# A gated linear unit over 32 tiles: the first tile's load split into four strided strips

## The chip, the core and the metric

The kernel runs on one core of a Trainium2 chip. Its time is the device time of one execution in microseconds (us). The median of three runs counts. Loads are issued by SyncE (SP), stores by ScalarE (ACT), and both kinds run on the core's 16 DMA engines.

## What is computed

`x` has 8192 rows of 8192 float32 numbers. Each row is cut in two halves, `a` and `b`, and the output has 8192 rows of 4096 numbers:

```python
def reference(x):
    a, b = np.split(x, 2, axis=-1)
    return a * (1 / (1 + np.exp(-b)))
```

That is a sigmoid and a product for each output number. 268.4 MB are read and 134.2 MB are written.

## The kernel before

A tile is 256 rows of `x`. Each of the 128 partitions takes two neighbouring rows (`R = 2`), which lie side by side in memory, so a tile is 128 runs of 64 KB, 8.39 MB in all. There are 32 tiles (`n_tiles`), and the loop of line 51 goes over them once. Two input buffers `x_sb` and two output buffers `o_sb` (`SLOTS = 2`) are used in turn, so even tiles share one pair and odd tiles the other.

For each tile, line 58 issues one load for all 128 partitions on SP's queue. Line 76 takes the sigmoid of the `b` halves in place on ScalarE, line 77 multiplies on VectorE into `o_sb`, and line 70 stores 4.19 MB on ACT's queue. For tiles 1 to 30 there is one sigmoid and one product for the whole tile; tile 0 and tile 31 are worked in four parts, and tile 31 is also stored in four parts of 1 MB. The load of tile i + 2 waits for the product of tile i, which has read the last of that buffer.

Two things stand outside of this order:

- Line 43 issues a small transfer, named `held`, as the first thing on ACT's queue. It reads 16 times 15 pieces of 64 bytes into a buffer `idle` that nothing uses. The stores go into the same queue behind it.
- `_launch_early` (line 99) works on the finished program: it takes the first load that stands on SP's queue and puts it ahead of the barrier with which all engines start.

`_close_on_sync` (line 112) rearranges the closing barrier so that the kernel ends on the completion of the last store. The calls of `implied` take out waits that follow from others.

Of the kernel before, what the change touches and what calls it, by code (L numbers as in the profile page):

```python
# [8 lines left out]
def _tiles(ctx, tc, x, out):  # L9

    nc = tc.nc
    P = nc.NUM_PARTITIONS  # L20
    DEP = mybir.DependencyInfo(mybir.DependencyClass.Sync, mybir.DependencyReason.DATA)
    fp32 = mybir.dt.float32
    SIG = mybir.ActivationFunctionType.Sigmoid

    n_rows, n_cols = x.shape
    half = n_cols // 2
    R = 2
    SLOTS = 2
    n_tiles = n_rows // (P * R)
    x_t = x.rearrange("(n p r) m -> n p (r m)", p=P, r=R)  # L30
    out_t = out.rearrange("(n p r) m -> n p (r m)", p=P, r=R)

    pool = ctx.enter_context(tc.tile_pool(name="io", bufs=1))
    xs = [pool.tile([P, R * n_cols], fp32, name=f"x_sb{k}") for k in range(SLOTS)]
    os = [pool.tile([P, R * half], fp32, name=f"o_sb{k}") for k in range(SLOTS)]

    def implied(later, *earlier):
        for e in earlier:
            tc.declare_no_dep(later.ins, e.ins, reason="follows from the waits that are kept")

    KEEP = 15
    idle = pool.tile([16, KEEP * 32], fp32, name="idle")
    held = nc.scalar.dma_start(
        out=idle.rearrange("p (k m) -> p k m", m=32)[:, :, 0:16],
        in_=x[0:16, 0 : KEEP * P].rearrange("p (k m) -> p k m", m=P)[:, :, 0:16],
    )
    tc.keep_in_program_order(held)

    gone = [{k: [] for k in ("loads", "sigs", "muls", "stores")} for _ in range(SLOTS)]
    last_stores = [[] for _ in range(SLOTS)]  # L50
    for i in range(n_tiles):
        old = gone[i % SLOTS]
        freed = last_stores[i % SLOTS]
        now = {k: [] for k in old}
        rows = xs[i % SLOTS].rearrange("p (r h m) -> p r h m", r=R, h=2)
        packed = os[i % SLOTS].rearrange("p (r m) -> p r m", r=R)

        load = nc.sync.dma_start(out=xs[i % SLOTS], in_=x_t[i])
        implied(load, *old["loads"], *old["sigs"])
        now["loads"].append(load)  # L60

        if 0 < i < n_tiles - 1:
            parts = [(slice(0, R), slice(0, half))]
        else:
            w = half // 2
            parts = [
                (slice(r, r + 1), slice(c * w, (c + 1) * w)) for r in range(R) for c in range(2)
            ]
        def store(cols):
            ins = nc.scalar.dma_start(out=out_t[i, :, cols], in_=os[i % SLOTS][:, cols])  # L70
            now["stores"].append(ins)

        chunks = []
        for k, (r, c) in enumerate(parts):
            b = rows[:, r, 1, c]
            sig = nc.scalar.activation(out=b, in_=b, func=SIG)  # L76
            mul = nc.vector.tensor_mul(out=packed[:, r, c], in0=rows[:, r, 0, c], in1=b)  # L77
            implied(sig, *old["sigs"], *old["muls"], *old["loads"])
            implied(mul, *old["muls"], *old["loads"], *now["loads"])
            by_sigmoid = i % 2 == 1 and len(parts) == 1  # L80
            implied(mul, *(s for s in old["stores"] if by_sigmoid or s not in freed))
            if by_sigmoid:
                for s in freed:
                    tc.add_manual_dep(sig.ins, s.ins.name, DEP, reason="frees the output slot")
            tc.keep_in_program_order(sig)
            now["sigs"].append(sig)
            now["muls"].append(mul)
            chunks.append(slice(r.start * half + c.start, r.start * half + c.stop))
            if i == n_tiles - 1 and k > 0:
                store(chunks[k - 1])  # L90
        store(chunks[-1] if i == n_tiles - 1 else slice(0, R * half))
        for s in now["stores"]:
            implied(s, *old["loads"], *old["sigs"], *old["muls"], *now["loads"], *now["sigs"])
        for k in old:
            old[k] += now[k]
        last_stores[i % SLOTS] = now["stores"]
# [71 lines left out]
@with_exitstack  # L168
def kernel(
    ctx: ExitStack,  # L170
    tc: tile.TileContext,
    x: bass.AP,
    out: bass.AP,
):
    nc = tc.nc
    with ExitStack() as pools:
        _tiles(pools, tc, x, out)
    tc.close()
    tc.compile()
    _launch_early(nc)  # L180
    _close_on_sync(nc)
# [30 lines left out]
```

## Time and profile before

| what | value |
|---|---|
| time, median of 3 runs | 933.45 us (933.36 to 933.45) |
| span of the profiled execution, first to last instruction | 931.9 us |
| what lies around the span (933.45 less 931.9) | 1.55 us |
| bytes moved by DMA, mean rate over the span | 402.68 MB, 432 GB/s |
| VectorE busy | 278.6 us, 30% of the span |
| ScalarE busy | 227.0 us, 24% of the span |
| loads: issue to landing, shortest, median, longest | 22.0, 42.2, 42.5 us |
| stores of 4 MB: issue to landing, median | 42.0 us |

The time of the profiled execution itself is not recorded beside the three runs; it is taken as its span and the 1.55 us around it, that is as the median. An engine's busy time is what it worked, not what it waited. The two compute engines are idle for two thirds of the span or more, and the DMA engines are busy throughout; a load's time from issue to landing holds the time that it stood in line behind another load.

### The profile page before, as it was taken

The numbers are of one execution on the slowest core, as the hardware profiler recorded it, in microseconds if no ns is written. First come the engines' busy times: TensorE is split into PE (matmuls) and PEld (weight loads), VectorE is DVE, ScalarE is ACT, GpSimd is POOL, SyncE is SP. The second block draws the span as 40 slices with busy tenths as digits, with TensorE's granted clock in tenths as the row PEclk, the third lists the DMA queues.
The fourth block names the chain that finished last, engine by engine and source line by source line (L and its number), as shares of the span: only waits on it lengthen the run. The fifth ranks groups of instructions, "written<-read, shape, count | busy, mean of one in ns | idle before, by whom it ended". The sixth has DMA issues, their size and how long they took to land.

```text
span 931.9 us, 249 instructions
## 1 busy us (share of the span) xinstructions
DVE 278.6 (30%) x38; ACT 227.0 (24%) x39; POOL 0.2 (0%) x4
## 2 busy tenths in 40 slices
DVE  0333312333123331133321333213332133321333
ACT  1413332133320333202332023320233202333023
POOL 0000000000000000000000000000000000000000
DMA  9999999999999999999999999999999999999999
GB/s 405 448 408 430 447 428 450 411 464 408 428 450 428 450 409 466 408 428 450 428 450 408 464 411 428 450 425 453 405 459 419 428 450 425 453 405 453 425 428 405
DMA packets 9905, 402.68 MB, mean 432 GB/s; under 512 B 1328, under 2 KB 1328, under 8 KB 1328
## 3 DMA queue, kind: packets, MB, share of 16 engines
q1 hardware_dynamic: 4608, 268.44, 66.6%
q10 hardware_dynamic: 5296, 134.24, 33.4%
q14 instruction: 1, 0.01, 0.0%
HBM read 268.45 MB, written 134.22 MB: 432 GB/s over the span
## 4 chain that ended last, share of the span: by engine, by line
DMA 72%; DVE 15%; ACT 12%; issue 0%; ACTq 0%
DMA x_sb<-in_x_dram 72%; DVE o_sb L77 15%; ACT x_sb L76 12%; ACTq L70 0%; ACTq L76 0%
## 5 line engine op out<-in xcount | busy, mean ns | idle before, releaser
L77 DVE TENSOR_TENSOR o_sb<-x_sb 128x8192 f32<-128x8192 f32 (+1 forms) x38 | 278.6, 7344 | 645.0 <-ACT x_sb L76 645.0
L76 ACT ACTIVATE x_sb<-x_sb 128x8192 f32<-128x8192 f32 (+1 forms) x38 | 225.7, 5950 | 693.2 <-DMA x_sb<-in_x_dram 691.9
L76 ACT ACT_TABLE_LOAD x1 | 1.3, 1283 | 1.2 <-PEq L196 1.2
L196 POOL MEMSET const-bfloat16-1.0<- 128x1 bf16 x1 | 0.1, 102 | 0.0
L196 POOL MEMSET const-uint8-127<- 128x1 uint8 x1 | 0.1, 101 | 0.0
L196 POOL MEMSET const-float32-0.0<- 128x1 f32 x1 | 0.1, 100 | 0.2 <-issue 0.2
L196 POOL MEMSET const-float32-1.0<- 128x1 f32 x1 | 0.1, 98 | 0.0
## 6 DMA issues: line engine op xcount, KB each, us to landing
out_dram<-o_sb ACTq DMA_DIRECT2D x31, 4096.0 KB, 42.0
out_dram<-o_sb ACTq DMA_DIRECT2D x4, 1024.0 KB, 7.9
x_sb<-in_x_dram SPq DMA_DIRECT2D x32, 42.2
idle<-in_x_dram ACTq DMA_DIRECT2D x1, 15.0 KB, 41.4
```

Source lines behind the costliest of these rows:

```text
L76: sig = nc.scalar.activation(out=b, in_=b, func=SIG)
L77: mul = nc.vector.tensor_mul(out=packed[:, r, c], in0=rows[:, r, 0, c], in1=b)
L196: nc = _bacc.Bacc("TRN2", target_bir_lowering=False, num_devices=1)
```

## The change

Tile 0 is loaded by four transfers where there was one. The first takes partitions 0, 8, 16, and so on to 120 (16 of them), the second partitions 4, 12, 20 and so on (16), the third partitions 2, 6, 10 and so on (32), and the fourth all odd partitions (64). Together they cover each partition once. `_launch_early` is unchanged, so it now moves the first of the four ahead of the barrier; the other three are issued behind the barrier, ahead of the load of tile 1. All other tiles are loaded as before.

```diff
-        load = nc.sync.dma_start(out=xs[i % SLOTS], in_=x_t[i])
-        implied(load, *old["loads"], *old["sigs"])
-        now["loads"].append(load)
+        steps = [(0, 1)] if i else [(0, 8), (4, 8), (2, 4), (1, 2)]
+        for at, step in steps:
+            p = slice(at, P, step)
+            load = nc.sync.dma_start(out=xs[i % SLOTS][p], in_=x_t[i, p])
+            implied(load, *old["loads"], *old["sigs"], *now["loads"])
+            now["loads"].append(load)
```

In the compiled program SP's queue gets three more issues, all of them ahead of the load of tile 1. On ScalarE, the first sigmoid of tile 0 waits for one of the four transfers and the loading of the sigmoid's table, which stands just ahead of it, now waits for the other three; before, it waited for none. The order on every other engine is the same, and lines behind the edit move down by three.

## The prediction

> **What bounds the kernel now.** I read the page first, then stretches of the run as a table, then the chain of waits and the timeline at both ends. From the page: the slices of DMA busy time, the queues, and the issues with their time from issue to landing.
>
> ```profile
> DMA  9999999999999999999999999999999999999999
> ...
> DMA packets 9905, 402.68 MB, mean 432 GB/s; under 512 B 1328, under 2 KB 1328, under 8 KB 1328
> ...
> q1 hardware_dynamic: 4608, 268.44, 66.6%
> q10 hardware_dynamic: 5296, 134.24, 33.4%
> ...
> out_dram<-o_sb ACTq DMA_DIRECT2D x31, 4096.0 KB, 42.0
> ...
> idle<-in_x_dram ACTq DMA_DIRECT2D x1, 15.0 KB, 41.4
> ```
>
> The DMA engines are never below nine tenths. q1 carries the loads: 4608 packets are 32 times 144, that is 128 rows of 64 KB and 16 completions for each load, so each of the 16 engines gets eight rows and one completion. q10 carries the stores and the small transfer. The 1328 packets under 512 B are its 240 pieces and 68 issues times 16 completions: a completion is a packet of its own.
>
> The next table is of stretches of the run: length, busy time of the engines, TensorE clock, DMA share, GB/s.
>
> ```profile
> 0.00:1.00 1.00, 0.00 (x0) 0.00 (x0) 0.20 (x4) 1.00 0.19 66
> 1.00:4.00 3.00, 0.00 (x0) 1.28 (x1) 0.00 (x0) 1.00 0.94 328
> ...
> 42.00:71.00 29.00, 8.69 (x1) 7.03 (x1) 0.00 (x0) 1.00 1.00 434
> 71.00:100.00 29.00, 8.69 (x1) 7.03 (x1) 0.00 (x0) 1.00 1.00 434
> 883.00:912.00 29.00, 8.69 (x1) 7.03 (x1) 0.00 (x0) 1.00 1.00 434
> ```
>
> One load and one store together take 29.0 us at a DMA share of 1.00, from the third tile to the last. The only loss that I see is at the start: 66 of 434 GB/s for 1 us and 328 for 3 us, worth 0.85 + 0.73 = 1.6 us. The end of the chain and the timeline's last store:
>
> ```profile
> 870.43 42.14 DMA x_sb<-in_x_dram
> 912.57 0.02 issue
> 912.59 1.92 ACT x_sb L76
> 914.51 0.02 issue
> 914.53 2.31 DVE o_sb L77
> ...
> 916.86 0.34 ACTq L70
> ```
>
> The last load lands at 912.57. What is left to store then is all of tile 30 (issued at 899.38, one product behind the landing of tile 30) and all of tile 31, 8.39 MB, and it takes 931.9 - 912.57 = 19.3 us: 434 GB/s again. So the tail is covered too. The chain names loads, sigmoids and products, but these are only the round trip of one buffer; the sum is made of DMA time. Whatever time the DMA engines lose at the start is added at the end, one for one, and nothing later gives it back.
>
> **The change, part by part.** *The bytes and rows* of tile 0 stay: 128 rows, eight to an engine if each strip is dealt evenly (1, 1, 2 and 4). *Three more issues* take SP 0.33 to 0.37 us each (the range of SP's 32 issues), 1.1 us in all. They stand ahead of the load of tile 1, which is not needed until tile 0 is through at 22 us, and of the load of tile 2, which waits until 32.89. One row is 64 KB on an engine, 2.42 us at 434 GB/s over 16, so the first strip covers the barrier and the second strip's issue. Price 0; without that cover 0.4 us for each issue.
>
> *A shorter first issue* is the gain. The whole tile's issue takes 0.37 us before the DMA can have all its rows; I take 0.3 us of that as won. The bounds are 0 and the whole starting loss of 1.6 us, which is below 0.2% of 933.45 (1.87 us), about what a measurement of this kernel can tell from no change.
>
> *The table load and its new waits.*
>
> ```profile
> 0.78 0.40 ACTq L43 DMA_DIRECT2D idle<-in_x_dram  x1
> 1.20 1.28 ACT L76 ACT_TABLE_LOAD   x1 [1.20 <-PEq L196]
> 22.03 7.31 ACT L76 ACTIVATE x_sb<-x_sb 128x2048 f32<-128x2048 f32 x4 [19.54 <-DMA x_sb<-in_x_dram]
> ```
>
> Now it follows the landing of tile 0, so tile 0's sigmoids, products, its store and the load of tile 2 (now at 32.9) come 1.3 us later. Queued behind the waiting instruction are only those and the later stores. The load of tile 2 is needed when tile 1 has landed, at 42.33: 9.4 us of cover. Price 0; without cover 1.3 us.
>
> *Three more completions on q1*, times 16 engines. This moves the stores. The small transfer is issued at 0.78 and lands 41.4 us later, together with the load of tile 1 (42.33): 15 KB cannot need that, so its 15 pieces and its completion go one at a time between packets of q1, and hold the store of tile 0 (issued at 32.90) back until tile 1 is in. Tile 0 and tile 1 are 18 packets of q1 on an engine before and 21 after. So the small transfer runs out three packets earlier, ahead of tile 1's last two or three rows, and up to three of the eight rows of tile 0's store go in between: 3 x 1.21 = 3.6 us later for the landing of tile 1, and of every tile behind it. The DMA does the same work in another order, so this costs nothing until the tail. There the work left over at the last landing falls from eight rows of tile 30 for each engine (9.7 us) to five (6.0 us). The first quarter's store is issued 916.86 - 912.57 = 4.3 us after the landing, and its data can flow 1.0 to 1.6 us later (as at the start), at 5.3 to 5.9: covered. Price 0, up to 1.1 us if a fourth row goes ahead (4.8 us left).
>
> *The strips themselves* are what I cannot read off. The limit is 434 GB/s with loads and stores mixed, 434 with stores alone in the tail, and 420 in the stretch from 5 to 20 us with loads alone. A limit that hardly cares for the direction is not one of reading or of writing memory; it sits at the DMA engines or between them and the 128 partitions. All transfers of weight in this trace cover all partitions, so no row tells the two apart. If it is the engines, the strips cost nothing. If it is paths that belong to groups of partitions, a strip that skips seven of eight partitions can leave paths idle while two engines share each of the others. Then its rows take 4.84 us instead of 2.42, and nothing else is queued to use the rest. The nearest row for the cost of a whole tile more is the second load, 42.33 - 22.03 = 20.3 us (with the small transfer's pieces in it); at the full rate it is 8.39 MB / 434 GB/s = 19.3 us. So the bounds are 0 and 20.3 us. Halved in the first two strips alone (a quarter of the rows) it is 19.3 / 4 = 4.8 us; halved in all four, 19.3 us. Between these ends I take 19.3: rows of a strip that go to an engine in sequence (0; 4; 2 and 6; 1, 3, 5, 7, each plus eight times its number) keep all four strips at the same spacing of eight partitions between engines, so what holds for one strip holds for the others.
>
> [...]
>
> **The sum.** Span 931.9 + 19.3 - 0.3 = 950.9; with the 1.55 us around it, 952.45, against the median of 933.45 that the same two terms give before. I say 952.4.
>
> **The rivals.** *No price* (not slower): the engines are the limit and stay evenly loaded. For it: rate and share are flat at 434 and 1.00 for whichever buffer, and each engine still gets eight rows. Then 933.45 - 0.3, with 0 to 1.1 for the tail: 933.1 to 934.6. It also holds if rows are dealt by partition, two of the first strip on each of eight engines; the other eight then start with the second strip, some 0.8 us later (the load of tile 1 was issued at 0.77), and the end is at 934.3. It decides if the first four rows of an engine still take about 10 us. *A quarter*: only the first two strips are halved and the larger ones are dealt as the whole tile is: 933.45 + 4.8 - 0.3 = 938.0. *More speed*: all of the starting loss gone, 931.9 at best, still within 0.2%; the rows exclude more. *Worse than half*, more than two engines on a path: nothing in the even spread of the strips over 0 to 127 suggests it.
>
> **How the numbers follow.** All strips halved 0.45, a quarter 0.17, no price 0.34, faster by over 0.2% 0.02, worse 0.02. So faster 0.02, same 0.34, slower 0.64. Since no single case reaches 8 in 10, the range goes from 933.0 to the bound of 20.3 us, 953.8; the likeliest case's own range is 950 to 953.8.
>
> **What would show it.** If I am right, the first 40 us run near 217 GB/s, tile 0 lands near 41 us and its first sigmoid starts near 42.5, tile 1 lands some 23 us later. q1 has 4656 packets. Stores take about 31 us from issue to landing instead of 42.0 (three rounds of 3.63 us less), and the last load lands 15 to 17 us ahead of the end, not 19.3. If tile 0 still lands near 22, the strips cost nothing and I am wrong by 19 us; near 27, only the first two do. If stores still take 42 us, the counting of completions is wrong.

## The result and the profile after

The changed kernel takes 937.94 us (median of 5 runs, 937.54 to 938.14) against 933.36 us of the kernel before in the same session: 4.58 us more, ratio 1.0048 with a 95% interval of 1.0036 to 1.006. The forecast was 952.4. The time agrees with the rival called *a quarter*, 938.0.

From the page of the changed kernel come the DMA slices, the load queue and the issues with their time to landing:

```profile
GB/s 314 426 459 437 406 468 403 448 426 426 448 426 427 447 448 410 463 403 451 423 428 445 448 426 424 449 412 440 428 459 412 428 444 449 426 424 449 417 434 403
...
q1 hardware_dynamic: 4656, 268.44, 66.8%
...
out_dram<-o_sb ACTq DMA_DIRECT2D x31, 4096.0 KB, 34.8
...
idle<-in_x_dram ACTq DMA_DIRECT2D x1, 15.0 KB, 6.9
```

Only the first slice is low (314 GB/s, where the kernel before has 405). The load queue has the 48 packets more that three more completions on 16 engines make. Two rows differ from what I expected: the stores land after 34.8 us, where I had forecast about 31 (42.0 before), and the small transfer after 6.9 us (41.4 before), where I had it run out only three packets earlier.

The table of stretches of the changed kernel (length, busy time of the engines, TensorE clock, DMA share, GB/s) shows where the time is lost:

```profile
1.00:11.00 10.00, 0.00 (x0) 0.00 (x0) 0.00 (x0) 1.00 1.03 211
11.00:26.00 15.00, 0.00 (x0) 0.00 (x0) 0.00 (x0) 1.00 1.00 419
26.00:49.00 23.00, 8.90 (x4) 8.59 (x5) 0.00 (x0) 1.00 1.00 433
...
42.00:71.00 29.00, 8.69 (x1) 7.03 (x1) 0.00 (x0) 1.00 1.00 434
```

The same 10 us of the kernel before:

```profile
1.00:11.00 10.00, 0.00 (x0) 1.28 (x1) 0.00 (x0) 1.00 1.01 413
```

For 10 us the DMA engines of the changed kernel are busy all the time (share 1.03) and move 211 GB/s; the kernel before moves 413. That is the time of the two strips of 16 partitions, 2.1 MB. The strips of 32 and 64 behind them run at 419 GB/s, and the steady state has the same 434 as before. So the DMA share here says nothing of the rate: it is 1.03 at 211 GB/s and 1.01 at 413. A row that takes 5.1 us counts as busy for all of that time, as one of 2.42 us does. In the trace's records of single rows of 64 KB, the first two on each engine take about 5.0 and 5.1 us, the third 2.6 to 3.2 (it begins while other engines are still at their second), and those that follow 2.42.

The timeline of the changed kernel at the start, ScalarE and the queues:

```profile
1.23 0.41 ACTq L43 DMA_DIRECT2D idle<-in_x_dram  x1
27.42 1.28 ACT L79 ACT_TABLE_LOAD   x1 [27.42 <-DMA x_sb<-in_x_dram]
28.71 7.31 ACT L79 ACTIVATE x_sb<-x_sb 128x2048 f32<-128x2048 f32 x4
...
39.58 0.37 ACTq L73 DMA_DIRECT2D out_dram<-o_sb  x1
49.14 7.03 ACT L79 ACTIVATE x_sb<-x_sb 128x8192 f32<-128x8192 f32 x1 [13.12 <-DMA x_sb<-in_x_dram]
```

Tile 0 is in at 27.42 instead of 22.03: 5.4 us later. The table load follows it, and the first sigmoid begins at 28.71. ScalarE leaves the barrier at 1.23, 0.45 us later than before.

### The profile page after: what moved, and what is told of

Same layout as the page of the kernel before. It is cut to its first block, busy times and chain, and to the rows that moved or that the text cites. A ratio compares the mean times of both kernels' runs of the same rounds, so it can differ in the third digit from the quotient of the medians.

```text
span 936.3 us, 256 instructions
## 1 busy us (share of the span) xinstructions
DVE 278.7 (30%) x38; ACT 227.0 (24%) x39; POOL 0.2 (0%) x4
## 3 DMA queue, kind: packets, MB, share of 16 engines
q1 hardware_dynamic: 4656, 268.44, 66.8%
## 4 chain that ended last, share of the span: by engine, by line
DMA 72%; DVE 15%; ACT 12%; issue 0%; SPq 0%; ACTq 0%
DMA x_sb<-in_x_dram 72%; DVE o_sb L80 15%; ACT x_sb L79 12%; SPq L61 0%; ACTq L73 0%; ACTq L79 0%
## 6 DMA issues: line engine op xcount, KB each, us to landing
out_dram<-o_sb ACTq DMA_DIRECT2D x31, 4096.0 KB, 34.8
```

## The experiments

Four theories were open. *Paths*, as the forecast assumed: groups of partitions share a path to the DMA engines, and a strip of 16 uses half of the paths. *One row*: a transfer that has one row for each engine is slow in itself. *Start*: the first rows of a run are slow. *Memory*: rows 512 KB apart are slow to read. The kernel before took 933.39 us beside the first four runs and 933.38 beside the last three.

**Blocks of neighbours.** The same sizes, but each strip is a block:

```diff
-        steps = [(0, 1)] if i else [(0, 8), (4, 8), (2, 4), (1, 2)]
-        for at, step in steps:
-            p = slice(at, P, step)
+        blocks = [(0, P)] if i else [(0, 16), (16, 32), (32, 64), (64, P)]
+        for lo, hi in blocks:
+            p = slice(lo, hi)
```

> Tile 0 in four blocks of neighbouring partitions (0 to 15, 16 to 31, 32 to 63, 64 to 127) in place of the four strided strips; as many rows for each engine and as many issues. Paths (groups of partitions share a path to the DMA engines): neighbours share more, so the rows of the first two blocks take longer than the 5.0 us of the strided strips, 7 to 10 us each, and the larger blocks, which ran at 2.42 us a row as strips, are slow as well: 4.8 us a row. Tile 0 then lands 25 to 30 us later than in the kernel before, and the time is 958 to 964 us. One row (a transfer with one row for each engine is slow in itself): 5.0 us for the first two rows and 2.42 us for the others, 938 us. Memory (rows that lie 512 KB apart are slow to read): rows now lie side by side, 2.42 us each, 933.5 us. [...]

Measured: 962.96 us in one run, 29.6 us more. The rows of the second block take 9.4 us, and those of the blocks of 32 and 64 partitions 5.0 to 5.1 us (but for the very first of them, 5.5 to 6.3, which begins while other engines are still at the second block). The landing of SP's first five issues, two stretches in the block of 64, and the timeline of this kernel:

```profile
DMA to landing us min/median/max: 12.1/30.4/71.3
```

```profile
30.00:35.00 5.00, 0.00 (x0) 0.00 (x0) 0.00 (x0) 1.00 1.01 210
35.00:40.00 5.00, 0.00 (x0) 0.00 (x0) 0.00 (x0) 1.00 1.03 210
```

```profile
51.82 1.28 ACT L79 ACT_TABLE_LOAD   x1 [51.82 <-DMA x_sb<-in_x_dram]
```

The first block of 16 lands after 12.1 us (the first strip of 16 of the changed kernel after 7.8), and all of tile 0 is in at 51.82. *One row* by itself falls: it has no reason why 16 rows, one on each engine, now take twice as long again, nor why the block of 64 runs at half the rate of the strip of 64. *Memory* falls as an explanation for these, since neighbours in memory are the slowest. *Paths* fits all four blocks: for it I had expected 7 to 10 us a row in the first two, 4.8 us in the larger ones, and 958 to 964 us in all; 8.7 and 9.4, 5.0 to 5.1 and 962.96 us were measured.

**Other memory, same partitions.** The two strips of 16 are filled from neighbouring rows of memory:

```diff
-            load = nc.sync.dma_start(out=xs[i % SLOTS][p], in_=x_t[i, p])
+            load = nc.sync.dma_start(
+                out=xs[i % SLOTS][p],
+                in_=x_t[i, slice(at * 4, at * 4 + 16) if step == 8 else p],
+            )
```

> The two strips of 16 partitions are filled from neighbouring rows of memory (runs 0 to 15 and 16 to 31 of the tile, 64 KB apart instead of 512 KB), so tile 0 holds the wrong rows in those partitions; partitions, sizes and issues are as in the changed kernel. Memory: the first two rows of an engine take 2.4 to 3.1 us, and the time falls to about 933.5 us. Paths and One row: they take 5.0 us as before, and the time stays at 937.5 to 938.2 us.

Measured: 937.79 us in one run, and in the table of stretches of this kernel the same halved rate:

```profile
5.00:10.00 5.00, 0.00 (x0) 0.00 (x0) 0.00 (x0) 1.00 1.06 213
10.00:15.00 5.00, 0.00 (x0) 0.00 (x0) 0.00 (x0) 1.00 1.06 419
```

The place in memory does not matter here: 937.79 us against the 937.94 of the changed kernel. The first two transfers of this kernel read the same rows of memory as the first two blocks above. By the trace's records their rows take 4.7 and 5.0 us here and 8.7 and 9.4 there, with only the partitions changed.

**The strips in the opposite order.**

```diff
-        steps = [(0, 1)] if i else [(0, 8), (4, 8), (2, 4), (1, 2)]
+        steps = [(0, 1)] if i else [(1, 2), (2, 4), (4, 8), (0, 8)]
```

> The same four strips in the opposite order: 64, 32, 16, 16 partitions. Start (the first rows of a run are slow, whatever they are): the four rows of the 64-partition strip now begin slowly, the 16-partition strips at the end take 2.42 us a row, and the first two rows take 5.0 us. Paths and One row: the 64 and 32 strips run at 2.42 us a row (the very first 3.0 us, as in the kernel before) and the two strips of 16 at about 4.8 us a row. The time is 937.5 to 938.3 us for both of these. The store of tile 0 is also looked at: if the small transfer ran out at once in the changed kernel because the load queue was empty for a moment when it arrived, it should here be spread over the rows again, as the first strip has four rows for each engine; the stores then land about 3 x 3.63 us earlier than 42.0 us, at 31 us, by the three more completions. If the early end has another reason they stay at 34.8 us.

Measured: 938.48 us, ratio 1.0055 (1.0038 to 1.0071), 0.2 us above the range that I expected. The stretches of this kernel:

```profile
1.00:16.00 15.00, 0.00 (x0) 0.00 (x0) 0.00 (x0) 1.00 1.02 420
16.00:26.00 10.00, 0.00 (x0) 0.00 (x0) 0.00 (x0) 1.00 1.01 223
```

The loss moves to the end of the tile with the two strips, so *Start* falls. Of the stores I had expected 31 us. The small transfer is indeed spread over the rows again (it lands after 39.0 us instead of 6.9), but the stores land after 36.9 us: tile 0's store is issued at 40.58 and its first row flows at 44.0, too late to put three rows ahead of the end of tile 1. The small transfer was out at 40.2, before that issue. So here the issue of the first store held it up, and the count of completions alone does not tell how far the stores get ahead.

**Eight strips of 16.** More of the suspected cost:

```diff
-        steps = [(0, 1)] if i else [(0, 8), (4, 8), (2, 4), (1, 2)]
+        steps = [(0, 1)] if i else [(k, 8) for k in range(8)]
```

> Eight strips of 16 partitions, starting at 0 to 7, each every eighth partition. Paths and One row: all eight rows of an engine take 4.8 to 5.1 us, so tile 0 lands about 20 us later than in the kernel before and the time is 951 to 954 us, the price that the forecast took for four halved strips. Start: only the first two rows are slow, 937 to 939 us.

Measured: 954.28 us in one run, 20.9 us more and 0.3 above the range that I expected; the whole of tile 0 comes at half rate:

```profile
1.00:21.00 20.00, 0.00 (x0) 0.00 (x0) 0.00 (x0) 1.00 1.03 210
21.00:42.00 21.00, 0.00 (x0) 1.28 (x1) 0.00 (x0) 1.00 1.02 218
```

This is the kernel whose price the forecast took.

**Three strips, and two.** No strip of 16 is left: from 0 and from 2 every fourth, then the odd ones; or even and odd partitions.

```diff
-        steps = [(0, 1)] if i else [(0, 8), (4, 8), (2, 4), (1, 2)]
+        steps = [(0, 1)] if i else [(0, 4), (2, 4), (1, 2)]   # three
+        steps = [(0, 1)] if i else [(0, 2), (1, 2)]           # two
```

> Three strips: every fourth partition from 0 (32 partitions), every fourth from 2 (32), all odd ones (64); the two strips of 16 are gone, all else is as in the changed kernel. Paths: strips of 32 and 64 ran at the full 2.42 us a row in the changed kernel, so nothing is halved now; tile 0 lands 0.3 to 0.7 us later than in the kernel before (the strided first issue takes 0.57 us instead of 0.37 and the barrier 0.45 us more), and the time is 933.0 to 934.2 us. If splitting itself had a price (three completions, three more issues, the table load behind the landing), 935 us or more stays.

> Two strips of 64, even and odd partitions. Paths with rows dealt by partition: no halving, 933.0 to 934.2 us as with three strips, and one completion and one issue less. If the strip of 64 ran at full rate in the changed kernel only because it came last, it would be slow as the first of the run: two to five us more.

Measured: 933.77 us with three (ratio 1.0006, 0.9997 to 1.0015) and 933.92 us with two (1.0007, 0.9998 to 1.0016): no difference from the kernel before that could be told. The first of the three strips, in the stretches of that kernel:

```profile
1.00:11.00 10.00, 0.00 (x0) 0.00 (x0) 0.00 (x0) 1.00 1.04 420
```

And with two strips, the even partitions first:

```profile
5.00:10.00 5.00, 0.00 (x0) 0.00 (x0) 0.00 (x0) 1.00 0.97 420
```

So the splitting, the one or two more issues and completions, and the table load behind the landing cost 0.4 to 0.5 us by the medians and at most 1.5 us by the intervals. The rest of the 4.58 us goes with the strips of 16. The comparison with the eight strips also says what the price hangs on. Partitions 0, 2, 4, ... come at full rate as one transfer of 64, and at half rate as four transfers of 16. It is not which partitions are loaded in the tile that counts, but which belong to one transfer. This fits *Paths* if the rows of a transfer of 32 or 64 are dealt so that no two engines are on one path for long. How they are dealt no run shows, nor the paths by themselves; what the runs show is the time of the rows.

One rival was not tested by itself. A transfer of 16 rows takes twice as long a row as a larger one of the same kind (5.0 against 2.42 us as strips, 9.4 against 5.1 as blocks), so a price on small transfers, beside one on neighbours, would give the same four numbers. No run has a transfer of 16 partitions spaced other than one or eight apart. The trace's records speak against this rival, because the time of a row there goes with what the other engines still have under way from another transfer. In the changed kernel the first row of the strip of 32 takes 3.15 us on the engine that begins it first (11.02), and less and less down to 2.63 on the one that begins it last (12.02), when the strips of 16 are through. With the opposite order, the engines that come to the first strip of 16 early need 4.45 to 4.55 us for its row and those that come last 4.9 to 5.0. A price that belongs to the small transfer itself would leave the first at 2.42 and make the second alike on all engines.

**Without the small transfer**, in the kernel before (lines 41 to 47 taken out):

```diff
-    KEEP = 15
-    idle = pool.tile([16, KEEP * 32], fp32, name="idle")
-    held = nc.scalar.dma_start(
...
-    tc.keep_in_program_order(held)
```

> The kernel before without the small transfer; nothing else is changed. The store of tile 0 may then flow from about 36 us, some two rows ahead of the end of tile 1's load, as in the changed kernel. Covered tail (my theory of the stores): which rows go first costs nothing as long as at least about 5.5 us of stores are left at the last landing, so the time is not worse than before: 932.3 to 933.6 us, with 4 MB stores landing in about 35 us. Rival: the small transfer's hold on the first store is worth its time, and without it the kernel loses 1 us or more (934.5 us and up).

Measured: 933.29 us, ratio 1.0002 (0.9993 to 1.0011), with the stores two rows earlier, as the page of this kernel says:

```profile
out_dram<-o_sb ACTq DMA_DIRECT2D x31, 4096.0 KB, 34.7
```

So the order of the first store's rows and tile 1's is worth nothing that can be measured (the interval allows 0.7 us less or 1.0 us more), with the tail covered as it is here (the last load is in about 17 us before the end of the span of 931.8). The small transfer's early end in the changed kernel puts the stores as far ahead, so it is not where the loss comes from.

No version beat both kernels: the best, without the small transfer, is level with the kernel before.

## Why the prediction was right or wrong

- **The step that failed: "Between these ends I take 19.3: rows of a strip that go to an engine in sequence".** The halving itself is there, and so is its size for a strip of 16 (rows of 5.0 and 5.1 us where I had 4.84, an estimate from twice the 2.42 of a row; that two engines share a path was my assumption and is not shown by a run). But I let the halving hold for all four strips, on the thought that larger strips are dealt to the engines in sequence, eight partitions apart. The strips of 32 and 64 ran at 2.42 us a row, so a quarter of the rows is halved: 4.58 us measured, 4.8 - 0.3 = 4.5 in the rival. That these agree within 0.1 us is in part luck: in the records the two halved rows cost 5.2 us, the start came 0.4 us later and not 0.3 earlier, and tile 1's rows gave 0.8 us back. The eight strips, 20.9 us, show what my term would have needed. I had the whole-tile load in hand as a counter-example: it has eight rows for each engine and runs at full rate, so its rows cannot be dealt in sequence eight partitions apart if paths belong to neighbours. That was a reason to trust the quarter more than the whole.
- **The DMA time adds up, one for one: right.** The steady state has 434 GB/s at the same share, and the loss of the first 11 us is found again at the end. In the trace's records, rows and pieces of all kinds take 5.8 us more in all than at their usual speed, for each engine, and 1.5 us in the kernel before; the 4.3 between them and 0.4 for the later start (below) make 4.7, near the 4.4 by which the spans differ (936.3 and 931.9). That nothing gives back lost time was not quite so: the rows of tile 1 take 0.8 us less than in the kernel before (last section).
- **A shorter first issue, 0.3 us won: wrong in sign.** The first issue of the strided strip of 16 takes 0.574 us, that of the whole tile 0.366 and that of the block of 16 neighbours 0.382. So the strided one is dearer, and fewer rows saved no time. The first row starts at 1.36 us instead of 1.00. The three more issues were mis-sized too: 0.50, 0.58 and 0.59 us instead of 0.33 to 0.37. Their price of 0 held, since the first strip's rows, the last of which ended at 6.8 us, covered them.

```profile
L61 SPq DMA_DIRECT2D x_sb<-in_x_dram x1: 574/574/574, 0.0 to 0.0; - x1
```

- **The table load behind the landing, price 0: right.** The load of tile 2 is issued when tile 0's last product is done, just ahead of the store at 39.58, and tile 1 lands at 49.14: 9.6 us of cover.
- **Three completions move the stores by three rows: partly.** There are 4656 packets, as counted. But the small transfer ran out at once, and the stores went two rows ahead (42.0 - 2 x 3.63 = 34.7, measured 34.8). Where it was spread over the rows, one more completion gave 38.4 us and two gave 37.3, and three gave 34.8 (blocks) and 36.9 (opposite order); the count says 38.4, 34.7 and 31.1. Only the first agrees. In the three kernels whose first strip is the strided strip of 16 it ran out in a burst, or nearly so (landing after 6.9, 6.9 and 21.8 us), and there its issue was through before that of the second strip (at 1.64 against 1.73 in the changed kernel). In the records of the kernel before, each engine runs its 15 pieces one at a time, each behind another packet of the load queue, from 6.5 to 38.7 us; in the changed kernel all run between 5.8 and 6.9 us. My reading is that the load queue had nothing to alternate with. That fits the traces of all kernels run; it was not tried by itself.
- **The tail is covered: right.** From the chain of the changed kernel:

```profile
877.12 42.04 DMA x_sb<-in_x_dram
...
919.19 1.92 ACT x_sb L79
...
923.45 0.34 ACTq L73
```

The last load lands at 919.17, 17.1 us before the end, where it was 19.3 (15 to 17 forecast): about two rows of 1.21 us. In the records, the first quarter's rows follow tile 30's last row without a gap.

- **Two sums among the rivals leave out the 0.3 us.** By its own terms *no price* is 933.2 to 934.3, not to 934.6, and its second form ends at 934.0, not 934.3. The forecast does not rest on them.

## What to carry to other kernels

In these runs, what counted when a transfer was cut up was which partitions belong to each piece, not only how many bytes each engine gets. One row for each engine, eight partitions apart, ran at half rate (211 GB/s, 5.0 and 5.1 us a row), 16 neighbours at about a quarter (8.7 and 9.4 us a row), blocks of 32 and 64 neighbours at half (5.0 to 5.1 us a row), and strips of 32 and 64 spread over all partitions at the full rate (419 GB/s, 2.42 us a row). In this kernel, whose DMA engines are never below nine tenths, such a loss at the start was paid at the end nearly in full (20.9 us for eight halved rows), while the waits and issues that stayed under the cover of a queued transfer cost 0.4 to 0.5 us by the medians of three and two strips, too little to be told from nothing. Price each piece of a split by itself: here what held for the strips of 16 (5.0 us a row) did not hold for the larger ones (2.42).

## What the runs showed that was not expected

- The first load was dearer to issue as a strided one: 0.574 us against 0.382 us for 16 neighbours, and the barrier that follows it comes 0.43 us later (ScalarE's first issue at 1.23 against 0.80). Strides are not the only cost of an issue: further back in the row of SP's issues, unstrided loads took as long (0.564 and 0.581 us for the fourth and fifth with the blocks, 0.587 for the load of tile 1 in the changed kernel). Why was not tried.
- A DMA share of 1.03 stood beside 211 GB/s, where the kernel before had 1.01 beside 413. The share alone did not tell that a transfer was held up.
- In the kernel before, the rows of tile 1 take 0.9 us more than usual on each engine, most of it in the row that runs on each engine just ahead of the first row of the first store (3.1 us instead of 2.42). It is there without the small transfer too (0.8 us), and not in the changed kernel nor with the opposite order. This gives back part of the 5.2 us that the halved rows cost; why it goes away was not tried.
